# Forgetting attention in a hybrid decoder block: maxima from one product, scores with keys on partitions

## The chip, the cores and the metric

The kernel is one program on one core of one Trainium2 chip. The metric is the device time of one execution in microseconds; shown are the median of three runs and one execution recorded by the hardware profiler. In the profile PE is the matrix engine, PEld its weight loads, DVE the vector engine, ACT the scalar engine, POOL the GpSimd engine and SP the engine that issues the DMAs.

## The reference

One decoder layer on x of shape (1, 2048, 1024) in float32. A normalised input is projected once, and the columns feed three branches: attention with forget gates (8 heads of 64), a chunked state-space branch, and a gated linear recurrence. Their outputs (512 + 1024 + 512 columns) are joined, multiplied by `w_out` (2048 x 1024) and added to x. What the change touches:

```python
q, k = rms_norm(q, q_g), rms_norm(k, k_g)            # per head, 64 wide
c = jnp.cumsum(log_f, axis=1)                        # one number per head and position
logits = q_i @ k.T * 64**-0.5 + (c_i[:, None] - ck[None, :])
logits = jnp.where(kpos <= qpos, logits, -jnp.inf)
o = jax.nn.softmax(logits) @ v
y_att = o * jax.nn.silu(z_att)
h = x + concat([y_att, y_ssd, y_lru]) @ w_out
```

## The kernel before

All large products are in float32r, which the kernel makes accurate by splitting an operand into a rounded part (`h`) and the rest (`l`) and adding products of the parts. The stages, in order of time: load and normalise x (transposed, split: `uh`, `ul`); projections of the state-space inputs with their convolution; the recurrence branch; the scan of the state-space branch beside the attention projections (`pqk`, `pvz`); attention; the last products with `w_out`. Results that a later stage needs go through DRAM (`qk_d`, `v_d`, `za_d`, `c_d`, `at_d`).

Attention works in units of one head `h` and 256 queries (`sb`, 0 to 7; 64 units, heads one after the other). A unit has sb+1 key pairs `kp` of 256 keys, so 36 per head and 288 in all. For a unit:

- `logits` (lines 855 to 905) takes each of its two blocks of 128 queries with queries on the partitions. For every chunk of up to 512 keys it makes two products (L880, L881: queries' large and small parts against both parts of the keys, stacked on the partitions), 320 chunks in all. A DVE instruction (L883) adds the cumulative gate, writes the logits to SBUF and keeps the running minimum of the negated logits; the diagonal chunk has its causal mask put on the gate rows by POOL (L875). One long exponential on ACT (L886) then runs over the whole row and gives the row sum.
- `attend` (lines 907 to 966) turns the probabilities by PE transposes of 128x128 (L936, 1088 in all) into PSUM, splits them into `ph` (ACT, L943) and `pl` (DVE, L944), and multiplies by the split values (L922, L923). At the end of a unit the result, head rows on partitions, is copied out, transposed back (L960), its two halves added and multiplied by the gate divided by the row sum (POOL, L913, L963, L964), and stored to `at_d` with positions as rows.
- The products of the next unit's logits are put between the key pairs of this unit.

The products with `w_out` are a generator, `sweeps`, with 512 steps of three products of 512 columns (L1006 to L1008, tile `po`). `fill` gives 260 of them to attention, about 0.9 after each key pair, and 12 to its start; they may come up to `LAG` = 4 pairs early. The other 240 steps follow attention. `mix` loads the left operand of a step; for the attention part it transposes what it reads from `at_d` (L984) before it splits it.

The order of instructions on each engine is fixed when the program is built, by a scheduler that works with estimated times and these priorities; on the chip every engine, and SP's queue of DMAs, runs in order.

The projection of values and attention gate (`group_vz`) makes products of 256 columns for head pairs 1 to 3 (L338, L340, L342) and of 280 for pair 0, with positions on partitions.

Of the kernel before, what the change touches and what calls it, by code (L numbers as in the profile page):

```python
# [13 lines left out]
ALU = mybir.AluOpType  # L14
# [23 lines left out]
AHEAD = 1  # L38
NDV = 3
# [7 lines left out]
def hybrid_block(ctx, tc, x, norm_g, w_in, q_norm_g, k_norm_g, forget_b, ssd_conv_w, ssd_conv_b,  # L47
# [16 lines left out]
    am = ctx.enter_context(tpool(name="am", bufs=4))  # L64
# [7 lines left out]
    v_d = [dram(f"v_d{p}", [S, 2, P]) for p in range(4)]  # L72
    za_d = [dram(f"za_d{p}", [S, P]) for p in range(4)]
# [6 lines left out]
    c_d = dram("c_d", [8, NT, P])  # L80
    gt_d = [dram(f"gt_d{g}", [4, P, S]) for g in range(2)]
    at_d = dram("at_d", [S, 512])
# [266 lines left out]
    def proj_ch(w, m, tb, name):  # L349
        wh, wl, n = w  # L350
        ps = psj.tile([P, 512], F32, name=name, tag="pj")
        ms = slice(m * P, m * P + P)
        for k in range(KD):
            T.matmul(ps, wh[k][:, ms], uh[tb][k], start=(k == 0), stop=False)  # L354
            T.matmul(ps, wh[k][:, ms], ul[tb][k], start=False, stop=False)  # L355
            T.matmul(ps, wl[k][:, ms], uh[tb][k], start=False, stop=(k == KD - 1))  # L356
        return ps


    def group_vz(pool, vpool, p):  # L360
        cols = [(C_V + p * P, P), (C_ZA + p * P, P)]
        if p == 0:
            cols += [(C_F, 8), (C_DT, 16)]
        w = weights(cols)
        for t2 in range(8):
            vs = vpool.tile([P, 2, 2, P], F32R, name=f"vs{p}_{t2}", tag="qk")
            zt = pool.tile([P, 2, P], F32, name=f"zt{p}_{t2}", tag="zt")
            if p == 0:
                pss = [proj_tok(w, t2 * 2 + i, f"pvz{p}_{t2 * 2 + i}")[:, 0:280].unsqueeze(1)
                       for i in range(2)]  # L370
            else:
                pss = [proj_tok2(w, t2, f"pvz{p}_{t2}")]
                if p == 3 and t2 == 4:
                    anchor[1] = anchor[0]
            m = 2 // len(pss)
            for j, ps in enumerate(pss):
                ii = slice(j * m, j * m + m)
                pv = ps[:, :, 0:P].rearrange("p i (h d) -> p i h d", d=64)
                A.activation(vs[:, ii, :, 0:64], pv, AF.Copy, scale=0.5)
                V.scalar_tensor_tensor(vs[:, ii, :, 64:128], pv, 0.5,  # L380
                                       vs[:, ii, :, 0:64].bitcast(F32), op0=ALU.mult,
                                       op1=ALU.subtract)
                th = (ap1 if p else pool).tile([P, m, P], F32, name=f"th{p}_{t2}_{j}",
                                               tag="sqq")
                A.activation(th, ps[:, :, P:2 * P], AF.Tanh, scale=0.5)
                V.scalar_tensor_tensor(zt[:, ii, :], th, 1.0, ps[:, :, P:2 * P], op0=ALU.add,
                                       op1=ALU.mult)
                if p == 0:
                    V.tensor_copy(etot[:, t2 * 2 + j, 0:8], ps[:, 0, 256:264])
                    V.tensor_copy(dt[:, t2 * 2 + j, :], ps[:, 0, 264:280])  # L390
            rr = slice(t2 * 256, t2 * 256 + 256)
            dma(v_d[p][rr].rearrange("(i p) h c -> p i (h c)", p=P),
                vs.bitcast(F32).rearrange("p i h c -> p i (h c)"))
            dma(za_d[p][rr, :].rearrange("(i p) c -> p i c", p=P), zt)
# [16 lines left out]
    def gates(g1):  # L411
# [62 lines left out]
        for t in range(NT):  # L474
            dma(c_d[:, t, :], cr[t * 8:(t + 1) * 8, :])
# [3 lines left out]
    with tpool(name="cl", bufs=1) as cl, tpool(name="g1", bufs=1, side="right") as g1:  # L479
        for gq in range(6):  # L480
            if gq == 1:

                group_vz(g0, g0, 0)
# [250 lines left out]
    cx = ExitStack()  # L734
    kvA = cx.enter_context(tpool(name="kvA", bufs=1, side="right"))
    kq = cx.enter_context(tpool(name="kq", bufs=2, side="right"))
    heads = {}
    units = [(h, sb) for h in range(8) for sb in ORD[h]]

    def load_head(h):  # L740
# [3 lines left out]
        kh = pool.tile([P, S], F32R, name=f"kh{h}", tag="kh")  # L744
        vv = pool.tile([P, NT, P], F32R, name=f"vv{h}", tag="vv")
        cb = pool.tile([P, S], F32, name=f"cb{h}", tag="cb")
        dma(cb, c_d[h:h + 1].rearrange("h t l -> h (t l)").partition_broadcast(P))
        dma(kh[0:64, :].bitcast(F32), qk_d["k", "h", p][hs, :])
        dma(kh[64:128, :].bitcast(F32), qk_d["k", "l", p][hs, :])
        dma(vv.bitcast(F32), v_d[p][:, b, :].rearrange("(t p) c -> p t c", p=P))  # L750
        heads[h] = [kh, vv, cb]


    def load_q(h, sb):
        p, b = divmod(h, 2)
        hs = slice(b * 64, b * 64 + 64)
        qh = kq.tile([P, 512], F32R, name=f"qh{h}_{sb}", tag="qh")
        ql = kq.tile([P, 512], F32R, name=f"ql{h}_{sb}", tag="ql")
        sb -= sb % 2
        qs = slice(sb * 256, sb * 256 + 512)  # L760
        for u in range(2):
            dma(qh[u * 64:u * 64 + 64, :].bitcast(F32), qk_d["q", "h", p][hs, qs])
            dma(ql[u * 64:u * 64 + 64, :].bitcast(F32), qk_d["q", "l", p][hs, qs])
        heads[h][3:] = [qh, ql]
# [30 lines left out]
    with tpool(name="ap", bufs=2) as pool, tpool(name="ap1", bufs=1) as ap1, \  # L795
            tpool(name="qkp", bufs=QB) as qkp:
        for p in range(4):
# [37 lines left out]
            if p > 0:  # L835
                group_vz(pool, qkp, p)
            if p == 2:
                load_head(0)
                load_q(*units[0])
# [4 lines left out]
    a4 = cx.enter_context(tpool(name="a4", bufs=4))  # L844
    o2 = cx.enter_context(tpool(name="o2", bufs=2))
    o3 = cx.enter_context(tpool(name="o3", bufs=LEAD))
    a2 = cx.enter_context(tpool(name="a2", bufs=2))
    a3 = cx.enter_context(tpool(name="a3", bufs=3))
    kvB = cx.enter_context(tpool(name="kvB", bufs=1))
# [3 lines left out]
    psP = pcx.enter_context(tpool(name="psP", bufs=PB[3], space=PSUM))  # L853

    def logits(h, sb):

        sm = a2.tile([P, 2], F32, name=f"sm{h}_{sb}", tag="sm")
        u = {"L": [], "sm": sm}
        steps = []

        def chunk(i, c0):
            kh, vv, cb, qh, ql = heads[h]
            u["vv"] = vv
            qt = sb * 2 + i
            n = (qt + 1) * P
            w = min(512, n - c0)
            if c0 == 0:
                u["L"].append(a4.tile([P, S], F32, name=f"L{h}_{qt}", tag="L"))
                u["mx"] = am.tile([P, 1], F32, name=f"mx{h}_{qt}", tag="mx")
            lt, mx = u["L"][i], u["mx"]  # L870
            last = c0 + w == n
            cc = cb[:, c0:c0 + w]
            if last:
                cm = a2.tile([P, 512], F32, name=f"cm{h}_{qt}", tag="cm")
                G.affine_select(out=cm[:, 0:w], in_=cc, pattern=[[-1, w]], compare_op=ALU.is_ge,  # L875
                                fill=-NEG, base=w - P, channel_multiplier=1)
                cc = cm[:, 0:w]
            qs = slice((sb % 2) * 256 + i * P, (sb % 2) * 256 + i * P + P)
            ps = psS.tile([P, 512], F32, name=f"S{h}_{qt}_{c0}", tag="S")
            T.matmul(ps[:, 0:w], qh[:, qs], kh[:, c0:c0 + w], start=True, stop=False)  # L880
            T.matmul(ps[:, 0:w], ql[:, qs], kh[:, c0:c0 + w], start=False, stop=True)  # L881

# [233 lines left out]
```

## Time and profile before

| | us |
|---|---|
| median of 3 runs (2053.45 to 2055.52) | 2053.6 |
| the profiled execution | 2056.6 |
| its span, first to last instruction | 2054.9 |
| PE busy in the span | 1997.6 |
| DVE busy | 1255.9 |
| ACT busy | 978.7 |
| POOL busy | 536.7 |

A busy time is the union of an engine's instructions. Matmuls are pipelined and their ends are modelled, so the time that a matmul costs is read from the distance between the starts of two that follow each other, not from its listed duration.

### The profile page before, as it was taken

What the parts mean: (1) busy time and instruction counts of PE and PEld (TensorE: products, weight loads), DVE (VectorE), ACT (ScalarE), POOL (GpSimd) and SP (SyncE); (2) the same over time, 40 slices, a digit from 0 to 9 for tenths busy, and PEclk for the clock granted to TensorE, in tenths of its full rate; (3) what the DMA queues carried; (4) which work ended last, traced back from release to release, by engine and by line L of the source; (5) the groups of instructions that cost most, each with busy time, mean ns of one, the idle gap of its engine ahead of it and who ended that gap; (6) DMA issues with size and microseconds to landing.
All of it is one profiled execution on the core that took longest, in us unless ns stands there. A gap on an engine that the chain in (4) does not pass through costs nothing. (4 is left out here: it accounts for less than half of the span.)

```text
span 2054.9 us, 36001 instructions
## 1 busy us (share of the span) xinstructions
PE 1997.6 (97%) x12517; PEld 1756.5 (85%) x12517; DVE 1255.9 (61%) x2676; ACT 978.7 (48%) x2049; POOL 536.7 (26%) x798
## 2 busy tenths in 40 slices
PE   7999999999999999898999999899999999999999
PEld 6898888898989898787888998788887888888887
DVE  5848555664554646767666255576776776784333
ACT  6624444444443534444445244466665666663110
POOL 0100000222232414455552001253333333323110
PEclk9999999999999999999999999999999999999999
DMA  5322223121212145667656646475476366442443
GB/s 187 85 74 70 63 82 96 44 73 32 83 39 87 30 123 162 187 179 209 196 160 182 179 143 194 142 204 161 135 188 174 113 181 169 119 136 86 134 143 118
DMA packets 287317, 265.18 MB, mean 129 GB/s; under 512 B 59780, under 2 KB 227232, under 8 KB 285088
## 3 DMA queue, kind: packets, MB, share of 16 engines
q1 hardware_dynamic: 286976, 262.85, 43.8%
q8 instruction: 99, 1.62, 0.3%
q0 software_dynamic: 160, 0.03, 0.1%
q14 instruction: 82, 0.67, 0.1%
HBM read 168.22 MB, written 94.57 MB: 128 GB/s over the span
## 5 line engine op out<-in xcount | busy, mean ns | idle before, releaser
L944 DVE TENSOR_TENSOR pl<-T,ph 128x512 fp32r<-128x512 f32 (+2 forms) x352 | 191.3, 565 | 71.4 <-ACT ph L943 69.7
L1006 PE MATMUL po<-woh,mh 128*128 128x512 f32 x512 | 213.2, 416 | 10.4 <-DVE xr L1014 6.6
L943 ACT CAST ph<-T 128x512 fp32r<-128x512 f32 (+2 forms) x352 | 161.6, 490 | 125.2 <-PE T L936 86.4
L1007 PE MATMUL po<-wol,mh 128*128 128x512 f32 x512 | 202.0, 395 | 0.0
L1008 PE MATMUL po<-woh,ml 128*128 128x512 f32 x512 | 201.2, 398 | 0.0
L936 PE MATMUL T<-ident,L 128*128 128x128 f32 x1088 | 171.5, 274 | 3.1 <-ACT L L886 2.1
L886 ACT ACTIVATE L<-L,mx 128x1920 f32<-128x1920 f32 (+15 forms) x128 | 154.5, 1207 | 40.6 <-DVE mx L883 36.5
L354 PE MATMUL pxx<-uh,wh 128*128 128x512 f32 x384 | 153.7, 402 | 2.2 <-ACT uh L299 2.1
L922 PE MATMUL O<-ph,vv 128*128 128x256 f32 x576 | 153.7, 288 | 0.6 <-ACT ph L943 0.5
L355 PE MATMUL pxx<-ul,wh 128*128 128x512 f32 x384 | 153.0, 400 | 0.0
L923 PE MATMUL O<-pl,vv 128*128 128x256 f32 x576 | 152.0, 288 | 0.5 <-DVE pl L944 0.3
L356 PE MATMUL pxx<-uh,wl 128*128 128x512 f32 x384 | 151.2, 396 | 0.0
L342 PE MATMUL pqk<-wh,ul 128*128 128x256 f32 x512 | 151.1, 295 | 0.0
L338 PE MATMUL pqk<-wh,uh 128*128 128x256 f32 x512 | 150.3, 294 | 0.0
L340 PE MATMUL pqk<-wl,uh 128*128 128x256 f32 x512 | 146.1, 285 | 0.0
L340 PE MATMUL pzs<-wl,uh 128*128 128x256 f32 x512 | 143.6, 281 | 0.0
L342 PE MATMUL pzs<-wh,ul 128*128 128x256 f32 x512 | 143.3, 280 | 0.0
L407 DVE SCALAR_TENSOR_TENSOR accx<-rtx,cv,accx 128x512 f32<-128x512 f32 x144 | 108.1, 752 | 57.4 <-ACT accx L404 54.4
L338 PE MATMUL pzs<-wh,uh 128*128 128x256 f32 x512 | 143.0, 281 | 0.0
L674 ACT ACTIVATE ab<-ab,nacs 128x128 f32<-128x128 f32 x256 | 82.1, 391 | 121.6 <-POOL ab L670 121.5
L936 PEld LDWEIGHTS T<-ident,L 128*128 128x128 f32 x1088 | 126.7, 141 | 14.3 <-ACT L L886 6.1
L875 POOL TENSOR_SCALAR_AFFINE_SELECT cm<-cb 128x384 f32<-128x384 f32 (+3 forms) x128 | 58.6, 460 | 298.5 <-DVE mx L883 144.6
(319 smaller groups left out, 5587.6 us busy)
## 6 DMA issues: line engine op xcount, KB each, us to landing
ab<-acs_d SPq DMA_DIRECT2D x64, 256.0 KB
pt_d<-xr SPq DMA_DIRECT2D x64, 256.0 KB
wr<-in_w_in_dram SPq DMA_DIRECT2D x192, 64.0 KB
wr<-in_w_in_dram SPq DMA_DIRECT2D x80, 128.0 KB
xt<-in_x_dram SPq DMA_DIRECT2D x16, 512.0 KB
xs_d<-stx SPq DMA_DIRECT2D x32, 256.0 KB
v_d<-vs SPq DMA_DIRECT2D x32, 256.0 KB
zs_d<-zs SPq DMA_DIRECT2D x32, 256.0 KB
```

The lines of the kernel that those rows point to most:

```text
L338: T.matmul(ps[:, i, :], h[k][:, sl], wh[k], start=(k == 0 and i == 0), stop=False, skip_group_check=True)
L340: T.matmul(ps[:, i, :], h[k][:, sl], wl[k], start=False, stop=False, skip_group_check=True)
L342: ins = T.matmul(ps[:, i, :], l[k][:, sl], wh[k], start=False, stop=last, skip_group_check=True)
L354: T.matmul(ps, wh[k][:, ms], uh[tb][k], start=(k == 0), stop=False)
L886: A.activation(lt[:, 0:n], lt[:, 0:n], AF.Exp, bias=mx, scale=-1.0, accum_out=sm[:, i:i + 1])
L922: T.matmul(po[:, ca], vv[:, kt, :], ph[:, jj, ca], start=(kt == 0), stop=False)
L936: ins = T.transpose(pt[:, jj, i * P:(i + 1) * P], L[i][:, kt * P:(kt + 1) * P], ident)
L943: A.copy(ph[:, ja, ca], pt[:, ja, ca])
L944: V.tensor_tensor(pl[:, ja, ca], pt[:, ja, ca], ph[:, ja, ca].bitcast(F32), op=ALU.subtract)
L1006: T.matmul(ps, mh[:, j, :], h, start=(j == 0), stop=False)
L1007: T.matmul(ps, mh[:, j, :], l, start=False, stop=False)
L1008: T.matmul(ps, ml[:, j, :], h, start=False, stop=(j == 3))
```

## The change

Queries and keys change places. The main steps:

- The row maxima come from one product per chunk instead of two, of the large parts only. The gate is part of that product: two rows of the keys' operand `k2` hold the split cumulative gate (`c_d` now holds both parts), against rows of ones in the queries' operand `q3`. A row of minus ones in `k2` and a row of `q3` for the maximum are used later. DVE reduces each chunk straight from PSUM (`maxima`); the diagonal chunk is masked by adding a constant tile.
- `flip` transposes the two columns of maxima of a unit and ACT writes them as rows into `q3`.
- `score` makes, for each key pair, the logits again with keys on partitions: two products of 256 query columns per 128 keys (`k2` with `q3`, and `kx` with `qx` for the small parts), minus the maximum; the diagonal pair gets its mask by one more product. ACT takes the exponential from PSUM, pair by pair, and copies the rounded part `ph`; DVE makes `pl`; POOL adds the probabilities up in `acc`. At the end of the unit POOL folds the sum to 256 columns, ACT and POOL split it.
- `av` multiplies by the values three pairs later (`AVL` = 3), and `finish`, one pair after the unit's last `av`, makes the row sums by two products with ones, adds the halves (ACT, DVE), multiplies by the gate (POOL) and stores heads and positions transposed. The row sums go to DRAM; in the last head they are read back, inverted and stored.
- `mix` for the attention part reads the transposed result and a broadcast of the inverse sums, and multiplies on DVE; its transposes are gone.
- `group_v` (values, two groups of 256 columns) and `group_za` (gate, transposed, products of 512 columns) replace `group_vz`.

The diff, cut to its core:

```diff
-    def logits(h, sb):
...
-    def attend(h, sb, u, steps, fill):
...
+    def maxima(j):
...
+        def first():
+            if j % 2 and j + 1 < len(units):
+                load_q(j + 1)
...
+        def chunk(i, c0):
...
+            T.matmul(ps[:, 0:w], q3[0:96, o:o + P], k2[0:96, c0:c0 + w], start=True, stop=True)
+            to = col if nc_ == 1 else u["mc"][:, c0 // 512:c0 // 512 + 1]
+            if c0 + w == n:
+                jk = a1.tile([P, 512], F32, name=f"jk{j}_{i}", tag="jk")
+                V.tensor_tensor_reduce(jk[:, 0:w], ps[:, 0:w], zm[:, 640 - w:640], 1.0, 3.0e38,
+                                       ALU.add, ALU.min, to)
+                if nc_ > 1:
+                    V.tensor_reduce(col, u["mc"][:, 0:nc_], axis=AX.X, op=ALU.min)
+            else:
+                V.tensor_reduce(to, ps, axis=AX.X, op=ALU.min)
...
+    def flip(j):
...
+        pm = psS.tile([P, P], F32, name=f"pm{j}", tag="S")
+        T.transpose(pm[0:97, :], mzs[j % 2][:, 0:97], ident)
+        A.copy(q3[96:97, o:o + P], pm[64:65, :])
+        A.copy(q3[96:97, o + P:o + 256], pm[96:97, :])
+
+    def score(j, kp):
...
+        for jj in range(2):
+            ks = slice((kp * 2 + jj) * P, (kp * 2 + jj + 1) * P)
+            qs = slice(o + P if last and jj else o, o + 256)
+            ps = pt[:, 256 * jj:256 * jj + qs.stop - qs.start]
+            T.matmul(ps, k2[:, ks], q3[:, qs], start=(jj == 0), stop=False, skip_group_check=True)
+            ins = T.matmul(ps, kx[:, ks], qx[:, qs], start=False, stop=True, skip_group_check=True)
+        if last:
+            pv = pt.rearrange("p (a b) -> p a b", b=256)[:, :, 0:P]
+            ins = T.matmul(pv, idr, zmt.unsqueeze(1).broadcast_to([P, 2, P]), start=False,
+                           stop=True, skip_group_check=True)
+        e = a4.tile([P, 512], F32, name=f"e{j}_{kp}", tag="e")
+        A.activation(e[:, 0:n], pt[:, 0:n], AF.Exp, scale=-1.0)
...
+        A.copy(ph[:, 0:n], e[:, 0:n])
+        V.tensor_tensor(pl[:, 0:n], e[:, 0:n], ph[:, 0:n].bitcast(F32), op=ALU.subtract)
...
+                G.tensor_tensor(u["acc"], u["acc"], e, op=ALU.add)
...
+            G.tensor_tensor(w, u["acc"][:, 0:256], u["acc"][:, 256:512], op=ALU.add)
+            G.tensor_tensor(w, w, e[:, 0:256], op=ALU.add)
...
+        G.tensor_tensor(w[:, P:256], w[:, P:256], e[:, 256:384], op=ALU.add)
...
+        A.copy(u["ah"], w[:, 0:256])
+        G.tensor_tensor(u["al"], w[:, 0:256], u["ah"].bitcast(F32), op=ALU.subtract)
...
+    def finish(j):
...
+        T.matmul(po[:, 256:512], onr, u["ah"], start=False, stop=False, skip_group_check=True)
+        T.matmul(po[:, 256:512], onr, u["al"], start=False, stop=True, skip_group_check=True)
...
+        A.copy(tm, po[64:128, :])
+        V.tensor_tensor(to, po[0:64, 0:256], tm[:, 0:256], op=ALU.add)
+        G.tensor_tensor(to, to, u["za"], op=ALU.mult)
...
+        dma(at_d[p][b * 64:b * 64 + 64, cs], to)
...
+        dma(s_d[qt, h:h + 1, :].rearrange("i o t -> o i t"),
+            tm[0:1, 256:512].rearrange("o (i t) -> o i t", i=2))
+        if h == 7:
+            sr = a2.tile([16, P], F32, name=f"sr{j}", tag="sr")
+            dma(sr, s_d[qt].rearrange("i h t -> (i h) t"))
+            V.reciprocal(sr, sr)
+            dma(r_d[qt].rearrange("i h t -> (i h) t"), sr)
...
         if kind == "att":
-            dma(mt.rearrange("p i c -> p (i c)"), at_d[tsl, :])
-            src = pso["X"].tile([P, 4, P], F32, name=f"px{t}_{k0}", tag="X")
-            for i in range(4):
-                T.transpose(src[:, i, :], mt[:, i, :], ident)
-            A.copy(mh, src)
-            V.tensor_tensor(ml, src, mh.bitcast(F32), op=ALU.subtract)
+            dma(mt, at_d[:, :, tsl].rearrange("i p t -> p i t"))
+            rb = o2.tile([P, 4, P], F32, name=f"rb{t}", tag="xr")
+            for b in range(2):
+                dma(rb[b * 64:b * 64 + 64, :, :],
+                    r_d[t].rearrange("(i b) t -> b i t", b=2)[b:b + 1].partition_broadcast(64))
+            V.tensor_tensor(mt, mt, rb, op=ALU.mult)
+            A.copy(mh, mt)
+            V.tensor_tensor(ml, mt, mh.bitcast(F32), op=ALU.subtract)
...
+    for i in range(len(tasks) + AVL + 1):
+        ins = None
+        if i < len(tasks):
+            ins = score(*tasks[i])
+            if i in flips:
+                flip(flips[i])
+            for f in at.get(i, ()):
+                f()
+        if 0 <= i - AVL < len(tasks):
+            av(*tasks[i - AVL])
+        if i > AVL:
+            j, kp = tasks[i - AVL - 1]
+            if kp == units[j][1]:
+                finish(j)
+        if ins is not None:
+            fill(ins)
```

`at` spreads the chunks of `maxima` of a unit over the pairs of the unit before; `flips` puts a unit's `flip` beside the last pair of the unit before. The tiles `e` have four buffers, `ph` and `pl` five, the score tiles in PSUM three, the tiles of `po` one as before.

More of the change, by code (lines that the diff above doesn't have):

```diff
@@ L38 @@
 AHEAD = 1
+AVL = 3
 NDV = 3
@@ L375, in group_vz @@
[L375 to L390, printed above, removed]
@@ new lines, in group_za @@
+    def group_za(pool, vpool, g):
+        w = weights([(C_ZA + g * 256, 256)])
+        for tb in range(4):
+            for mm in range(2):
+                m = g * 2 + mm
+                ps = proj_ch(w, mm, tb, f"pza{m}_{tb}")
+                if g == 1 and tb == 2 and mm == 0:
+                    anchor[1] = anchor[0]
+                th = pool.tile([P, 512], F32, name=f"th{m}_{tb}", tag="sqq")
+                A.activation(th, ps, AF.Tanh, scale=0.5)
+                zt = vpool.tile([P, 512], F32, name=f"zt{m}_{tb}", tag="qk")
+                V.scalar_tensor_tensor(zt, th, 1.0, ps, op0=ALU.add, op1=ALU.mult)
+                dma(za_d[m][:, tb * 512:(tb + 1) * 512], zt)
@@ L853, in hybrid_block @@
     psP = pcx.enter_context(tpool(name="psP", bufs=PB[3], space=PSUM))
-    def logits(h, sb):
-        sm = a2.tile([P, 2], F32, name=f"sm{h}_{sb}", tag="sm")
-        u = {"L": [], "sm": sm}
-        steps = []
[L861 to L881, printed above, removed]
-            V.tensor_tensor_reduce(lt[:, c0:c0 + w], ps[:, 0:w], cc, 1.0,
-                                   3.0e38 if c0 == 0 else mx, ALU.add, ALU.min, mx)
-            if last:
-                A.activation(lt[:, 0:n], lt[:, 0:n], AF.Exp, bias=mx, scale=-1.0,
-                             accum_out=sm[:, i:i + 1])
@@ L889, in first @@
+    make_k2(1)
+    U = [{} for _ in units]
+    def maxima(j):
+        h, sb = units[j]
+        u = U[j]
+        steps = []
         def first():
-            j = units.index((h, sb))
-            if j % 2 == 0 and j > 0:
-                load_q(h, sb)
-            za = a2.tile([P, 2, 64], F32, name=f"za{h}_{sb}", tag="za")
+            if j % 2 and j + 1 < len(units):
+                load_q(j + 1)
+            za = a3.tile([64, 256], F32, name=f"za{j}", tag="za")
             u["za"] = za
@@ new lines, in av @@
+    def av(j, kp):
+        h, sb = units[j]
+        u = U[j]
+        vv = heads[h][2]
+        if kp == 0:
+            u["O"] = psO.tile([P, 512], F32, name=f"O{j}", tag="O")
+        po = u["O"]
+        ph, pl = u.pop(kp)
+        for jj in range(2):
+            kt = kp * 2 + jj
+            qs = slice(P if kp == sb and jj else 0, 256)
+            cs = slice(256 * jj, 256 * jj + 256 - qs.start)
+            T.matmul(po[:, qs], vv[:, kt, :], ph[:, cs], start=(kt == 0), stop=False,
+                     skip_group_check=True)
+            T.matmul(po[:, qs], vv[:, kt, :], pl[:, cs], start=False, stop=(kt == 2 * sb + 1),
+                     skip_group_check=True)
@@ L1059, in hybrid_block @@
     with tc.high_priority(offset=HP), tc.issue_after(anchor[1].ins):
-        cur, steps = logits(*units[0])
+        steps = maxima(0)
         for j, st in enumerate(steps):
@@ L1075, in fill @@
                 next(filler)
[L1077 to L1080 removed]
+    tasks = [(j, kp) for j, (h, sb) in enumerate(units) for kp in range(sb + 1)]
+    begin = [tasks.index((j, 0)) for j in range(len(units))]
+    at = {}
+    for j in range(1, len(units)):
+        a, b = max(0, begin[j - 1] - 1), begin[j] - 1
+        st = maxima(j)
+        for i, f in enumerate(st):
+            at.setdefault(a + i * (b - a) // len(st), []).append(f)
+    flips = {begin[j] - 1: j for j in range(1, len(units))}
+    for i in range(len(tasks) + AVL + 1):
[14 more added lines that the diff above has]
+            fill(ins)
     pcx.close()
[L1082 to L1083 removed]
+    pso["P"] = cx.enter_context(tpool(name="psP2", bufs=6, space=PSUM))
+    pso["X"] = True
     for _ in filler:
```

243 lines of the change are left out of this document (136 added, 107 removed).

## The prediction

> **What bounds the kernel now.** First the page: the span, how busy PE is, the chain that ended last, and the group that the change breaks up.
>
> ```profile
> span 2054.9 us, 36001 instructions
> ...
> PE 1997.6 (97%) x12517; PEld 1756.5 (85%) x12517; DVE 1255.9 (61%) x2676; ACT 978.7 (48%) x2049; POOL 536.7 (26%) x798
> ...
> PE 43%; DVE 2%; DMA 2%; issue 1%; ACT 1%; POOL 0%; SPq 0%; DVEq 0%; POOLq 0%; ACTq 0%
> ...
> L886 ACT ACTIVATE L<-L,mx 128x1920 f32<-128x1920 f32 (+15 forms) x128 | 154.5, 1207 | 40.6 <-DVE mx L883 36.5
> ```
>
> PE is busy nearly throughout, and the chain names it above all others, so the time is first of all a count of matmuls. Next, the busy times by stage: attention, and what follows it.
>
> ```profile
> 1292.00:1885.00 593.00, 582.67 (x3706) 509.83 (x3705) 428.12 (x1164) 370.09 (x770) 205.64 (x407) 0.99 0.53 150
> 1885.00:2055.00 170.00, 165.72 (x756) 135.75 (x756) 56.40 (x132) 16.61 (x28) 17.14 (x14) 1.00 0.39 132
> ```
>
> The columns are length, then PE, PEld, DVE, ACT and POOL busy, then clock and DMA. In the 593 us of attention PE is idle for 10 us, at a clock of 0.99; DVE is busy 72%, ACT 62%, POOL 35%. The 170 us after it are products with w_out alone. What a matmul costs there is read from starts in PE's timeline (start, then listed duration):
>
> ```profile
> 1303.52 0.28 PE L922 MATMUL O<-ph,vv 128*128 128x256 f32 x1
> ...
> 1304.58 0.28 PE L923 MATMUL O<-pl,vv 128*128 128x256 f32 x1
> 1304.70 0.60 PE L936 MATMUL T<-ident,L 128*128 128x128 f32 x4
> 1305.05 0.48 PE L1006 MATMUL po<-woh,mh 128*128 128x512 f32 x1
> 1305.37 0.40 PE L1007 MATMUL po<-wol,mh 128*128 128x512 f32 x1
> 1305.60 0.40 PE L1008 MATMUL po<-woh,ml 128*128 128x512 f32 x1
> ```
>
> Ten products of 256 columns start between 1303.52 and 1304.70: 0.118 us each. One of 512 takes 0.23 (1305.37 to 1305.60). The four transposes and the two products after them take 0.90 up to 1305.60; less 2 x 0.23 that is 0.111 for a transpose of 128, nearly the price of 256 columns. The first product behind them starts late, so the transposes' own starts alone would make them too cheap.
>
> **The change on PE.** Counts follow from the loops; these rows confirm the two largest.
>
> ```profile
> L936 PE MATMUL T<-ident,L 128*128 128x128 f32 x1088 | 171.5, 274 | 3.1 <-ACT L L886 2.1 <-DVE pl L944 0.8
> ...
> L881 PE MATMUL S<-kh,ql 128*128 128x512 f32 x224 | 88.9, 397 | 0.0
> ```
>
> Removed:
> - the second product of 320 chunks: 224 x 0.23 + 32 x (0.173 + 0.118 + 0.111) = 64.4;
> - 1088 transposes of probabilities x 0.111 = 120.8;
> - two transposes per unit, 128 x 0.111 = 14.2;
> - in the products after attention 4 x 16 transposes = 7.1;
> - 768 projections of 256 columns become 384 of 512: 90.6 - 88.3 = 2.3.
>
> Sum 208.8. Added:
> - scores, four products per pair, 1152, of which 128 are half as wide: 1024 x 0.118 + 128 x 0.111 = 135.0;
> - the mask, 64 x 0.118 = 7.6;
> - the transpose of the maxima, 64 x 0.111 = 7.1;
> - row sums, 128 x 0.118 = 15.1.
>
> Sum 164.8. Net: PE has 44.0 us less to do, 35 of them in attention. The products with values stay at 1152, the steps with w_out at 512. Two of these have no row. A product over 96 partitions instead of 128 could be cheaper by a quarter (320 x up to 0.06 = 18 less) or not at all; I take not at all, as the rows show a price by columns. The mask product reads its operand repeated and writes in two pieces: 0.118, at most 0.23, so 7 more.
>
> **The change on DVE.** Rows for a read of PSUM with one operand in SBUF, for two operands in SBUF while POOL works, and for two in SBUF over twice the columns:
>
> ```profile
> L944 DVE TENSOR_TENSOR pl<-T,ph 128x512 fp32r<-128x512 f32 x224 | 148.8, 687 | 58.8 <-ACT ph L943 57.4
> ...
> L690 DVE TENSOR_TENSOR y<-y,yo 128x512 f32<-128x512 f32 x30 | 25.3, 845 | 0.5
> ...
> L621 DVE TENSOR_TENSOR XC<-XC,MM 128x1024 f32<-128x1024 f32 x8 | 9.8, 1226 | 6.4 <-ACT MM L618 6.3
> ```
>
> The 320 reductions of chunks stay 320 reads of PSUM of the same widths: 0. `pl` now reads both operands from SBUF: between 0.613 (half of 1.226) and 0.845 instead of 0.687, so for 224 full ones -17 to +35. New are 64 additions of 256 columns at the end of units, some 0.42 each (an estimate from half of 0.687), 27 us, and 96 very short reductions of at most 0.26, 25 us. DVE goes from 428 to between 463 and 515.
>
> **The change on ACT.**
>
> ```profile
> L943 ACT CAST ph<-T 128x512 fp32r<-128x512 f32 x224 | 123.6, 588 | 66.4 <-PE T L936 60.6 <-PE O L922 3.0 <-DVE pl L944 1.6
> ...
> L956 ACT COPY os<-O 128x256 f32<-128x256 f32 x64 | 23.6, 368 | 23.1 <-PE O L923 22.5 <-ACT L L886 0.2
> L993 ACT CAST mh<-mt 128x512 fp32r<-128x512 f32 x36 | 22.3, 621 | 15.7 <-PE po L1007 8.2 <-DMA kh<-kh_d 2.5 <-DMA mt<-gt_d 2.4
> L943 ACT CAST ph<-T 128x128 fp32r<-128x128 f32 x64 | 16.8, 263 | 31.6 <-DVE pl L944 31.5
> ```
>
> Gone: the long exponentials, 154.5, and two copies per unit, 128 x 0.368 = 47. New: 288 exponentials from PSUM, priced as the cast from PSUM, 224 x 0.588 + 64 x 0.46 = 161, up to a fifth more; `ph` from SBUF, 224 x (0.621 - 0.588) = 7; `tm`, 64 x 0.588 = 38; `ah`, 64 x 0.368 = 24; two rows of maxima per unit, 128 x at most 0.263 = 34. Net +62 to +94: ACT goes from 370 to 432 to 464.
>
> **The change on POOL.** It gets the sums of probabilities:
>
> ```profile
> L994 POOL TENSOR_TENSOR ml<-mt,mh 128x512 fp32r<-128x512 f32 x48 | 62.0, 1292 | 202.2 <-ACT mh L993 178.7 <-PE O L922 13.6 <-PE pf L960 4.4
> ...
> L682 POOL TENSOR_TENSOR xs<-xs,drow 128x512 f32<-128x512 f32 x32 | 35.4, 1108 | 0.3
> L192 POOL TENSOR_TENSOR wl<-wr,wh 128x256 fp32r<-128x256 f32 x32 | 32.2, 1010 | 121.9 <-ACT wh L191 121.8
> ...
> L963 POOL TENSOR_TENSOR ats<-fs 128x128 f32<-128x128 f32 x64 | 29.4, 460 | 116.9 <-ACT fs L962 97.9 <-DMA at_d<-ats 16.9 <-DVE sm L910 1.1
> ...
> L583 POOL TENSOR_TENSOR ZZ<-tzl,ZZ 128x512 f32<-128x512 f32 x16 | 21.4, 1342 | 0.4
> ```
>
> A head has 21 additions of 512 columns to `acc`: 168 x 1.108 to 1.342 = 186 to 225. Folding, in 56 units: twice 256 columns, at 0.676 (on the line from 0.460 to 1.108) to 1.010, and once 128 at 0.460: 101 to 139; 8 x 0.46 = 4 in the rest. The split `al` and the gate, 64 each of 256 columns: 86 to 130. The splits for w_out in the stage, 35 x 1.292 = 45. POOL goes from 206 to between 422 and 543.
>
> **Waits.** With PE's 35 us gone, attention would take 558. DVE would be busy 83 to 92% of that, ACT 77 to 83%, POOL 76 to 97%: the covers are thinner than before. A product with values now comes three pairs behind its scores, the score tiles in PSUM have three buffers and are read by ACT alone, and `finish` comes four pairs behind the last score, some 7 us: I cost these at nothing, hidden by PE's work on pairs in between. A pair is 0.47 for scores, 0.47 for values, 0.9 x 3 x 0.23 = 0.62 for w_out and 0.2 for chunks of maxima, 1.8 in all.
>
> What is late next is the first score of a unit. It waits for its maxima: the last reduction 0.69, a short one 0.26, the transpose 0.27 (its listed duration), two casts 0.53, and one instruction ahead on DVE (0.69) and one on ACT (0.59): 3.0 us. Ahead of it on PE's queue stand the values and w_out of one pair; behind it everything else. A long unit before it covers that. Where the unit before has one or two pairs (16 of 64), 3.0 - 1.8 = 1.2 us is open: 19 us. The old kernel had the same kind of chain through L883, L886 and L936 and yet lost little, so nothing is the lower bound; 64 units x 1.2 = 77 the upper. I take 19, since the rows say that most units are long.
>
> `load_q` now writes one of two fixed tiles, free only when the unit two before has made its last score; in seven heads the unit between has one pair, 1.8 us. The queue rows, from SP's own list of waits, show what a wait for a DMA costs it:
>
> ```profile
> SPq L1027 <- DMA pt_d<-xr: 62.6, 45, 4.2
> ```
>
> At 4.2 each that is 7 x 2.4 = 17, at the mean of 1.4 nothing. I take nothing. The last head adds, per unit, a store of sums, a read back and a store: 8 x 3 x 1.4 = 34 us in which SP's queue stands, with loads for w_out behind it. These are asked for one tile of eight steps ahead, some 16 us, so nothing; without that cover the first steps after attention wait once, 3 x 4.2 = 13. Three DMAs for queries instead of four and the two rows of gates instead of a broadcast are lighter: nothing.
>
> **Sum.** The profiled execution took 2056.6, 1.7 over its span; the median is 2053.6, 3.0 under it. Its own time less 44 plus 19 is 2031.6; for the median, 2053.6 - 44 + 19 = 2029.
>
> **The rivals.**
>
> *Slower: POOL waits for ACT within each unit's fold.* `ah` on ACT follows POOL's fold, `al` on POOL follows `ah`, and both engines run in order; behind `ah` on ACT stand the next exponentials, behind `al` the next additions, and the four buffers of `e` come free only with them. POOL's waits for a copy by ACT:
>
> ```profile
> POOL ats L963 <- ACT fs L962: 97.9, 41, 7.0
> ```
>
> That is 2.4 us each; 64 x 2.4 = 153. With POOL's middle, 480, the stage would be 633, with its lowest 575, which PE hides. It decides from 593 + 9 = 602 on (9 is what PE saves outside attention). Halfway between 602 and 633 the time is 2053.6 - 9 + 25 = 2070. Against it: these old waits were idle time of an engine with nothing to do, and `al` has four pairs.
>
> *DVE and POOL shut each other out.* L690 takes 0.845 beside a busy POOL, where L621 needs 0.613 for as many columns. If `pl` and POOL exclude each other entirely, their least prices add: 224 x 0.613 + 64 x 0.46 = 167, and 422, together 589. Attention then takes 589 instead of 593: 2053.6 - 9 - 4 = 2041, and with 3% of gaps 2058. The Trainium skill ("SBUF — State Buffer", section "SBUF: two separate sides") states such a rule: a DVE instruction with two SBUF operands and a GpSimd instruction that reads SBUF hold one pair of ports in turn, each for its whole length. The two rows agree in direction; that POOL's instructions at 1.108 were not all uncontended themselves speaks against the full sum.
>
> *All of it arrives.* No new wait, and the 10 us of idle time go as well: 2053.6 - 44 to 54, so 2000 to 2010, up to 2016. For it: values now have three pairs of slack instead of one. Against it: three engines above 75%.
>
> **How the numbers follow.** The forecast (2016 to 2041) 0.43; all of it (2000 to 2016) 0.18; exclusion (2041 to 2058) 0.15; POOL and ACT (2058 to 2085) 0.22; others 0.02. A measurement of this kernel tells 0.2%, 4 us, from no change. Faster: 0.43 + 0.18 + 0.06 of exclusion, 0.67; same: its other 0.09; slower: 0.22 + 0.02. The range, 2005 to 2072, leaves out a third of the full gain's chance and less than half of the slow case's. The forecast's own range is 2016 to 2041.
>
> **What would show it.** Right: 576 fewer matmuls in all (11941), attention near 577, scores and values starting 0.118 apart, PE's idle time in front of the first score of short units, released by ACT. Wrong: POOL near 95% with ACT's `ah` waiting for it (the slow rival); `pl` at 0.85 or more and POOL's additions over 1.3 (exclusion); DVE ahead of PE in the chain; PE waiting for the loads of queries. What would break the forecast is a PE that is no longer the engine others wait for.

## The result and the profile after

The changed kernel takes 2213.9 us (median of 4 runs, 2201.7 to 2218.6), the kernel before 2054.6 beside it: ratio 1.0765, 95% interval 1.0725 to 1.0805. It is 159 us slower; the forecast was 2029, and the range ended at 2072. From the page of the changed kernel: span, busy times, the chain by engine and by line, and two groups (busy time, mean ns, idle time before).

```profile
span 2200.0 us, 34666 instructions
...
PE 2048.2 (93%) x11941; PEld 1762.5 (80%) x11941; DVE 1433.3 (65%) x2513; ACT 1019.2 (46%) x2113; POOL 880.2 (40%) x898
...
PE 18%; DVE 9%; POOL 4%; issue 3%; DMA 2%; ACT 2%; SPq 0%; DVEq 0%; POOLq 0%; ACTq 0%
DVE pl L986 5%; PE po L1095 4%; PE po L1096 4%; PE po L1097 4%; PE T L974 2%; PE T L975 2%; POOL ac L996 1%; DVE mc L942 1%; PE S L932 1%; PE O L1026 1%; DVE jk L937 1%; DMA at_d<-to 1%; ACT e L982 1%; POOL w L1001 1%; POOL w L1000 1%
...
L986 DVE TENSOR_TENSOR pl<-e,ph 128x512 fp32r<-128x512 f32 (+1 forms) x288 | 338.2, 1197 | 46.4 <-ACT ph L985 46.2
...
L996 POOL TENSOR_TENSOR ac<-ac,e 128x512 f32<-128x512 f32 x120 | 185.9, 1549 | 23.2 <-ACT e L982 16.1
```

The 11941 matmuls are those predicted. The chain covers only part of the span, 49% before and 38% now; of what it covers PE had 43 of 49 before and has 18 of 38 now, and its costliest line is now `pl` on DVE. The mean of `pl`, 1197 ns, mixes 512 and 384 columns; by form, the full ones take 1299. The windows of attention and of what follows, columns as before:

```profile
1285.00:2040.00 755.00, 649.12 (x3592) 546.59 (x3592) 591.48 (x1024) 415.88 (x863) 528.52 (x493) 0.92 0.40 110
2040.00:2200.00 160.00, 155.51 (x687) 128.47 (x685) 63.40 (x145) 16.80 (x27) 15.84 (x12) 1.00 0.51 158
```

All of the loss lies in attention, 755 us instead of 593, with PE idle for 106 of them and at a granted clock of 0.92 instead of 0.99. What follows is shorter than before, 160 instead of 170, and so is what precedes it, 1285 instead of 1292. The list of waits (engine, tile and line, releaser: us, times, longest) of attention and its start names the candidates:

```profile
ACT ah L1007 <- POOL w L1004: 125.1, 46, 5.7
...
PEld O L1026 <- DVE pl L986: 73.2, 99, 3.1
...
PE O L1026 <- DVE pl L986: 47.9, 68, 2.9
```

And the timeline (start, length of the group of instructions) shows `pl` beside POOL's additions:

```profile
1641.32 6.23 POOL L996 TENSOR_TENSOR ac<-ac,e 128x512 f32<-128x512 f32 x4 [0.85 <-ACT e L982]
...
1642.93 5.18 DVE L986 TENSOR_TENSOR pl<-e,ph 128x512 fp32r<-128x512 f32 x3
```

Three `pl` take 5.18 us while POOL adds without a pause, and four additions take 6.23. One after the other, by the least prices of the prediction, they would take 3 x 0.613 + 4 x 1.108 = 6.27. But 1.108 is the price of another POOL instruction; the same additions take 1.30 where `pl` is out of their way (e1), and with 1.30 the sum is 7.04, against 5.2 for the four additions alone. So the two run nearly in turn, with a part of each overlapped.

So three theories: A, `pl` and POOL's additions shut each other out, and PE waits for `pl`; B, ACT's `ah` waits for POOL's fold (125 us, the larger wait); C, the new products cost PE more than priced.

### The profile page after: what moved, and what is told of

Its sections match the earlier page's. It is cut to its first block, busy times and chain, and to the rows that moved or that the text cites. A ratio compares the mean times of both kernels' runs of the same rounds, so it can differ in the third digit from the quotient of the medians.

```text
span 2200.0 us, 34666 instructions
## 1 busy us (share of the span) xinstructions
PE 2048.2 (93%) x11941; PEld 1762.5 (80%) x11941; DVE 1433.3 (65%) x2513; ACT 1019.2 (46%) x2113; POOL 880.2 (40%) x898
## 5 line engine op out<-in xcount | busy, mean ns | idle before, releaser
L986 DVE TENSOR_TENSOR pl<-e,ph 128x512 fp32r<-128x512 f32 (+1 forms) x288 | 338.2, 1197 | 46.4 <-ACT ph L985 46.2
L1026 PE MATMUL O<-pl,vv 128*128 128x256 f32 x576 | 162.9, 313 | 48.8 <-DVE pl L986 47.9
L982 ACT ACTIVATE e<-T 128x512 f32<-128x512 f32 (+1 forms) x288 | 162.8, 575 | 85.5 <-PE T L975 48.4
L996 POOL TENSOR_TENSOR ac<-ac,e 128x512 f32<-128x512 f32 x120 | 185.9, 1549 | 23.2 <-ACT e L982 16.1
L1026 PEld LDWEIGHTS O<-pl,vv 128*128 128x128 f32 x576 | 114.8, 199 | 76.3 <-DVE pl L986 73.2
L974 PE MATMUL T<-q,k 128*128 128x256 f32 x576 | 163.2, 305 | 12.9 <-ACT q L958 12.5
L942 DVE TENSOR_REDUCE mc<-S 128x1 f32<-128x512 f32 x192 | 129.9, 682 | 57.8 <-PE S L932 57.6
L985 ACT CAST ph<-e 128x512 fp32r<-128x512 f32 (+1 forms) x288 | 165.3, 597 | 2.8 <-PE O L1024 0.6
L1083 POOL TENSOR_TENSOR ml<-mt,mh 128x512 fp32r<-128x512 f32 x48 | 67.1, 1399 | 244.1 <-ACT mh L1082 244.0
L975 PE MATMUL T<-qx,kx 128*128 128x256 f32 x576 | 156.6, 299 | 0.0
```

The lines of the kernel that those rows point to most:

```text
L974: T.matmul(ps, k2[:, ks], q3[:, qs], start=(jj == 0), stop=False, skip_group_check=True)
L975: ins = T.matmul(ps, kx[:, ks], qx[:, qs], start=False, stop=True, skip_group_check=True)
L982: A.activation(e[:, 0:n], pt[:, 0:n], AF.Exp, scale=-1.0)
L985: A.copy(ph[:, 0:n], e[:, 0:n])
L986: V.tensor_tensor(pl[:, 0:n], e[:, 0:n], ph[:, 0:n].bitcast(F32), op=ALU.subtract)
L996: G.tensor_tensor(u["acc"], u["acc"], e, op=ALU.add)
```

## The experiments

### Where the 159 us went: e1 to e4

**e1_pl_psum.** `pl` takes its first operand from the score tile in PSUM instead of `e` in SBUF; everything else stays, so POOL has the same work.

```diff
-        V.tensor_tensor(pl[:, 0:n], e[:, 0:n], ph[:, 0:n].bitcast(F32), op=ALU.subtract)
+        V.tensor_tensor(pl[:, 0:n], pt[:, 0:n], ph[:, 0:n].bitcast(F32), op=ALU.min)
```

> DVE's instruction for pl takes its first operand from the score tile in PSUM instead of e in SBUF (and the smaller of the two instead of their difference, to keep numbers finite): the values are not those of the reference, the number and width of instructions and all of POOL's work stay. Theory A (pl and POOL's additions shut each other out, because both read two operands from SBUF): pl falls from 1.20 us on average to about 0.69, POOL's additions from 1.48 to 1.1 to 1.3, PE's 121 us of waits for pl nearly vanish, time 2030 to 2100. Theory B (ACT's ah waits 125 us for POOL's fold and holds up what is behind it): pl changes little in what PE waits for, time 2150 or more. Theory C (the new products cost PE more than their starts say): time stays within 20 of 2202.

2114.3 us (one run), 100 less, a little short of the 2030 to 2100 expected by theory A. Its page, and PE's waits:

```profile
L986 DVE TENSOR_TENSOR pl<-T,ph 128x512 fp32r<-128x512 f32 (+1 forms) x288 | 186.3, 655 | 67.5 <-ACT ph L985 66.9
...
L996 POOL TENSOR_TENSOR ac<-ac,e 128x512 f32<-128x512 f32 x120 | 155.5, 1296 | 33.1 <-ACT e L982 29.0
```

```profile
PEld O L1026 <- DVE pl L986: 10.7, 17, 1.3
```

One operand moved to the other memory takes `pl` from 1197 to 655 and POOL's additions from 1549 to 1296 at once, and PE's weight loads wait 10.7 us for `pl` instead of 73.2. Theory A holds.

**e2_no_sums.** The same conflict, taken away on POOL's side: the 168 additions to `acc` go. The row sums are then those of the last two key pairs alone, and eight short DVE instructions, left out of the diff here, keep them above zero.

```diff
-            if kp == 0:
-                u["acc"] = e
...
-                G.tensor_tensor(u["acc"], u["acc"], e, op=ALU.add)
+            u["acc"] = e
             return ins
```

> The 168 additions of probabilities into acc on POOL are left out (the row sums are then those of the last two key pairs, so the output is not the reference's; a guard keeps them above zero); the fold, ah and al stay. Theory A: with POOL's work halved pl falls to 0.65 to 0.80, time 2030 to 2090, close to the run with pl from PSUM. Theory B: the fold is no longer late, ah's wait for POOL falls from 125 to under 40 us, time 2030 to 2090 too; the two are told apart by the other runs. Theory C: within 20 of 2202.

2142.5 us (one run), 71 less.

```profile
L986 DVE TENSOR_TENSOR pl<-e,ph 128x512 fp32r<-128x512 f32 (+1 forms) x288 | 218.9, 775 | 70.9 <-ACT ph L985 70.3
```

`pl` falls with its own instruction unchanged, to a mean inside theory A's 0.65 to 0.80, because POOL has less to read. The time missed that theory's 2030 to 2090: the folds and `al` remain on POOL, and `pl` stays above e1's 655. The same cause, from the other side.

**e3_ah_early.** Theory B: `ah` is copied from the last `e`, ahead of POOL's fold, so that ACT never waits for POOL there.

```diff
+        A.copy(u["ah"], e[:, 0:256])
         if sb > 0:
             w = a2.tile([P, 256], F32, name=f"w{j}", tag="w")
...
-        A.copy(u["ah"], w[:, 0:256])
```

> ah is copied from the last pair's e, ahead of the fold, so ACT does not wait for POOL (al = w - ah still makes the sum whole); the rest is unchanged. Theory A: ACT's 125 us of waiting go, but pl stays at 1.1 us or more and PE goes on waiting for it: time 2150 to 2200. Theory B: time 2050 to 2100. Theory C: within 20 of 2202.

2219.2 us (one run): no gain, even 19 us over what theory A expected. The largest wait of the list is gone from it, and the time is where it was; PE still waits for `pl`:

```profile
PEld O L1026 <- DVE pl L986: 62.7, 91, 4.0
```

Theory B falls. ACT stands elsewhere instead: over the whole span its waits for PE ahead of `q` grew from 72.1 to 125.7, and those ahead of `tm` from 23.2 to 81.4.

**e4_exp_in_psum.** The conflict removed with the computation kept: the exponential is written in place in PSUM, `ph` and `pl` read it there, and POOL sums `ph`, the rounded value that PE uses.

```diff
-        A.activation(e[:, 0:n], pt[:, 0:n], AF.Exp, scale=-1.0)
+        A.activation(pt[:, 0:n], pt[:, 0:n], AF.Exp, scale=-1.0)
...
-        A.copy(ph[:, 0:n], e[:, 0:n])
-        V.tensor_tensor(pl[:, 0:n], e[:, 0:n], ph[:, 0:n].bitcast(F32), op=ALU.subtract)
+        A.copy(ph[:, 0:n], pt[:, 0:n])
+        V.tensor_tensor(pl[:, 0:n], pt[:, 0:n], ph[:, 0:n].bitcast(F32), op=ALU.subtract)
+        e = ph.bitcast(F32)
```

> The exponential is written back into the score tile in PSUM, ph and pl are made from it there, and POOL adds up the rounded ph from SBUF instead of e (row sums of the rounded part). pl keeps one operand in SBUF. Theory A: pl about 0.69, POOL's additions 1.1 to 1.3, time 2030 to 2100 although the score tiles are held longer. Theory B: ah still waits for the fold, 2150 or more. Theory C: within 20 of 2202.

2115.3 us (median of 2), ratio to before 1.0292 (1.0224 to 1.0359): 98.6 us of the 159 are gone, somewhat less than theory A had promised, as in e1.

```profile
L985 DVE TENSOR_TENSOR pl<-T,ph 128x512 fp32r<-128x512 f32 (+1 forms) x288 | 186.3, 655 | 68.9 <-ACT ph L984 65.9
...
L996 POOL TENSOR_TENSOR ac<-ac,ph 128x512 f32<-128x512 f32 x120 | 155.8, 1299 | 14.6 <-ACT ph L984 9.2
```

`pl` and POOL both read the tile `ph` here, at the speed of e1, so it was not that they shared a tile. But 61 us are still lost against before. The waits of attention in this kernel:

```profile
PE pm L956 <- DVE mz L940: 27.8, 22, 4.8
```

```profile
ACT tm L1042 <- DMA s_d<-tm: 30.1, 6, 6.7
```

The six waits of ACT lie in six heads, each 12 to 16 us behind the loads of the next head. One of them in the timeline, SP's queue first:

```profile
1351.23 7.36 SPq L1047 DMA_DIRECT2D at_d<-to  x1
```

```profile
1363.66 0.58 ACT L1042 COPY tm<-O 64x512 f32<-64x512 f32 x1 [6.70 <-DMA s_d<-tm]
```

```profile
1350.00:1370.00 20.00, 14.78 (x72) 12.24 (x70) 9.59 (x25) 8.97 (x20) 8.92 (x14) 0.83 0.80 185
```

Five loads of the next head are issued up to 1350.64. The store behind them, normally 0.5 us, takes 7.36 to issue (in the other five heads it is a load of queries that stands there, for 6.5 to 9.3 us); the store of the sums stands behind it; `tm` has two buffers, so ACT stands 6.70 in front of the next `tm`, and the exponentials of units that begin stand behind `tm`. PE is busy 14.78 of 20 us, at a clock of 0.83. Two theories for the rest: S, this queue; F, the flip chain (maxima on DVE, transpose on PE, two copies on ACT) ahead of each unit's first score.

### Where the other 61 us went: e5 to e8

**e5_tm_bufs.** e4 with four buffers for `tm` and `to`.

```diff
-        tm = a2.tile([64, 512], F32, name=f"tm{j}", tag="tm")
-        to = a2.tile([64, 256], F32, name=f"to{j}", tag="to")
+        tm = a4.tile([64, 512], F32, name=f"tm{j}", tag="tm")
+        to = a4.tile([64, 256], F32, name=f"to{j}", tag="to")
```

> The kernel with the exponential in place in PSUM (2115.3 us), with four buffers instead of two for tm and to. In its trace ACT stood 30.1 us in front of tm for the store of an earlier tm, six times 6.7 us, at the heads' starts, and a store of at_d took 7.36 us to issue on SP behind the next head's loads. Theory S (stores held up on SP stop ACT, and ACT stops the exponentials and flips behind tm): the 30 us of ACT's wait go, and with a clock that falls less after the gaps, 2075 to 2095. Theory F (the flip chain, from the row maxima on DVE over PE's transpose to the two copies on ACT, holds every unit's first score; the stores stand beside it): 2105 to 2118.

2077.4 us, ratio 1.0107 (1.0079 to 1.0136): 37.9 less than e4, as theory S said. How long the stores of `at_d` took to issue (least/median/most, ns), and who waited for the store of the sums:

```profile
L1047 SPq DMA_DIRECT2D at_d<-to x64: 458/494/7327, 1289.7 to 1910.2; - x64
```

```profile
  ACT tm L1042: 3.1, 1
```

The slow issue is still there, 7.3 us; the buffers only keep ACT from standing behind it. PE's waits for `mz`, 27.8 in e4, fell too, though nothing of the flip was changed:

```profile
PE pm L956 <- DVE mz L940: 10.3, 19, 2.0
```

**e6_load_later.** e4 with the next head's loads at the sixth unit of a head instead of the third.

```diff
-            if j % 8 == 2 and h < 7:
+            if j % 8 == 5 and h < 7:
```

> The same kernel (2115.3 us) with the next head's loads issued three units later, away from the short units that begin a head. Theory S: SP's queue is free when the short units store, so the 30.1 us of ACT's wait before tm go, or move to where units are long and cost little: 2075 to 2100. Theory F: 2105 to 2118.

2116.1 us, ratio 1.0284 (1.0255 to 1.0313): no gain over e4, the number of theory F. But the block is not gone, it moved with the loads:

```profile
ACT tm L1042 <- DMA s_d<-tm: 30.7, 5, 8.3
```

So what theory S forecast here failed, 2075 to 2100 with the waits gone or cheap; but the block that it names is still there, with the same wait of ACT. The remedy missed it: it isn't the short units that make the block. That five loads at once make it is tried in e9.

**e7_maxima_early.** e4 with the maxima two pairs and the flip one pair earlier (a third `q3` tile and more buffers of `qx`; the loads go one unit later, to keep their place in the order).

```diff
-        a, b = max(0, begin[j - 1] - 1), begin[j] - 1
+        a, b = max(0, begin[j - 1] - 3), begin[j] - 3
...
-    flips = {begin[j] - 1: j for j in range(1, len(units))}
+    flips = {begin[j] - 2: j for j in range(1, len(units))}
```

> The same kernel (2115.3 us) with each unit's row maxima two pairs earlier and its flip one pair earlier (a third q3 tile, a third qx buffer; the next head's loads stay at the same place in the order). Theory F: PE's waits for mz in front of pm (27.8 us, 22 of them) and for ACT's q in front of the first scores (10.8 us, 25 of them) go, and the time comes to 2065 to 2085. Theory S: the gaps are made by ACT standing in front of tm, and a flip that is issued earlier stands behind it in the same way: 2100 to 2118.

2093.5 us, ratio 1.0188 (1.0169 to 1.0207): 21.8 less than e4, between the two expectations. PE's waits for `mz` in front of `pm` shrank from 27.8 to 5.0, those for `q` in front of the first scores from 10.8 to at most 1.1, and a new one took part of their place, the PSUM bank of `pm` being held until ACT has copied it; the block at `tm` stayed:

```profile
PE S L936 <- ACT q L962: 30.7, 26, 5.9
```

```profile
ACT tm L1046 <- DMA s_d<-tm: 38.9, 6, 7.7
```

**e8_all.** All of these: exponential in PSUM, three buffers for `tm` and `to`, loads at the sixth unit, maxima and flips earlier.

> All of it together: exponential in place in PSUM, three buffers for tm and to, head loads later, maxima and flips earlier. If exclusion, stores and flip chain are the whole of the gap, PE has nothing left to wait for: 2015 to 2045, which is 10 to 40 below the kernel before. If PE's own work costs more than the sum of my prediction (2010 to 2029), or the granted clock stays at 0.86 to 0.95 in the attention with PE busy, it stops at 2060 to 2090, and the change can't win by mending waits.

2072.5 us, ratio 1.0079 (1.0058 to 1.0101). That is the number of the second case, a PE that can't win, but not by its reason, as e9 and e11 show. The two gains don't add: 37.9 and 21.8 alone, 42.8 together. One gap, in the timeline of SP and of DVE and in the windows, shows what is left:

```profile
1363.92 6.47 SPq L1053 DMA_DIRECT2D s_d<-tm  x1
```

```profile
1377.62 0.42 DVE L1110 TENSOR_TENSOR xr<-xr,po 128x256 f32<-128x256 f32 x1 [5.70 <-DMA mt<-lr_d]
```

```profile
1370.00:1380.00 10.00, 3.63 (x25) 3.21 (x23) 3.68 (x10) 1.70 (x5) 4.99 (x6) 0.88 0.87 220
```

SP's queue still stands 6.5 us behind the five loads. ACT no longer cares; now DVE does, in front of an `xr` of the products with w_out. The row names the load `mt<-lr_d`, which was issued at 1375.50, behind the store that stood; a load of an `xr`, at 1373.58, was too. The maxima stand behind that `xr`, and PE waits 6.37 us for them. It is busy for 3.63 of 10 us. A queue that blocks finds the next engine to block.

### The queue itself, and a version below before: e9 to e12

**e9_loads_spread.** e8 with the five loads spread over five units (the keys and their gate rows in the first, the values in two halves).

```diff
-            if j % 8 == 5 and h < 7:
-                load_head(h + 1)
+            if j % 8 >= 3 and h < 7:
+                load_head(h + 1, j % 8 - 3)
```

> The kernel with all four edits (2072.5 us) with the next head's loads no longer issued together but one for each of five units (the values in two halves). In its trace 1360 to 1370 had a DMA share of 0.92, one store took 6.47 us to issue on SP, an xr on DVE stood 5.7 us for a load that came after it, and PE 6.4 us for the maxima behind that xr. Theory S (SP's queue full at heads' starts): seven heads by some 6 us, with the clock that falls after it: 2025 to 2060. Theory P (PE is near its own sum, its many short waits remain): 2065 to 2075.

2059.3 us (median of 10), ratio 1.002 (1.0004 to 1.0037): 13.2 below e8, just inside what theory S expected. The longest issue of a store of the sums, 6.47 us in e8, is now 1.83:

```profile
L1061 SPq DMA_DIRECT2D s_d<-tm x64: 585/602/1831, 1291.9 to 1890.3; - x64
```

But the queue is not free of blocks. The longest issue of any DMA in attention falls from 9.02 to 4.13, that of a load behind a head whose loads were still issued within 8 us (1421 to 1429):

```profile
1429.94 4.13 SPq L1094 DMA_DIRECT2D mt<-lr_d  x1
```

**e10_values_later.** The products with values 4 pairs behind the scores (six buffers for `ph` and `pl`); to make room, `tm` and `to` go back to two buffers.

```diff
-AVL = 3
+AVL = 4
```

> The same with loads spread, two buffers for tm and to again, and the products with the values 4 pairs behind the scores instead of 3 (six buffers for ph and pl). Theory P: PE's waits for pl in front of the products with values, 7.5 + 3.7 us in the kernel with all four edits, go: 5 to 15 us below the kernel with loads spread. If SP is relieved, the third buffer of tm and to is not missed; if it is, the time is 10 to 30 above it.

2082.4 us, ratio 1.0125 (1.0105 to 1.0145): 23 above e9, inside the 10 to 30 expected if the third buffer is missed.

```profile
ACT tm L1054 <- DMA s_d<-tm: 27.4, 5, 6.9
```

ACT's wait for the store is back. In one of its five places (6.44 us, up to 1436.01) the queue still blocks: the store of the sums is issued at 1433.50, behind this load:

```profile
1428.23 5.18 SPq L1094 DMA_DIRECT2D mt<-lr_d  x1
```

In the other four no issue took over 2.8 us, and the store lands late all the same: one issued by 1597.26 lets ACT go on at 1601.92. So it isn't the issue alone that the third buffer covers. What `AVL` alone does stays open: two things were altered in one run.

**e11_banks.** e9 with three PSUM banks for the maxima and two for the scores.

```diff
-PB = (2, 3, 2, 1)
+PB = (3, 2, 2, 1)
```

> The same as the kernel with loads spread, with three PSUM banks for the maxima and two for the scores, instead of two and three. PE waited 20 us for the copies q before it could start a product of the maxima (the bank of pm). If these waits hold PE, the time falls by 5 to 20 us; if the scores' banks do, since ph and pl now read them to the end, it rises by 30 or more.

2050.5 us (median of 9), ratio to before 0.9976 (0.996 to 0.9993): 8.8 below e9, as expected for the bank of `pm`, and the one version faster than before, by 0.24%, less than what single runs of either kernel differ by. Its attention and what follows, and PE's largest wait in attention:

```profile
1292.00:1887.00 595.00, 561.42 (x3556) 502.15 (x3557) 437.74 (x1014) 422.81 (x857) 449.42 (x501) 0.97 0.50 140
1887.00:2050.00 163.00, 159.14 (x703) 131.51 (x701) 66.79 (x150) 17.42 (x28) 16.82 (x13) 0.99 0.49 155
```

```profile
PE S L944 <- DMA q<-qh_d: 12.3, 9, 3.8
```

The waits for `q` on ACT are gone from the top; the largest is now for the loads of queries. Its three longest, 3.85, 3.46 and 2.32 us, each follow a block of SP's queue, the first this one:

```profile
1427.10 6.96 SPq L813 DMA_DIRECT2D qx<-qh_d  x1
```

```profile
1441.06 0.77 PE L944 MATMUL S<-k,q 96*128 96x512 f32 x1 [3.85 <-DMA q<-qh_d]
```

The loads of the next head, spread over five units in the code, were issued within 4 us there (1421.57 to 1425.4). So the fastest version still has the blocked queue, and what a queue without it would give was not run.

**e12_after_spread.** The changed kernel as it was given, with the loads spread and nothing else.

> The changed kernel as it was given (2213.9 us), with nothing altered but the next head's loads spread over five units. Theory A (pl and the additions of POOL shut each other out, which is about 100 of the 159 us): 2180 to 2205. If the loads at the heads' starts make the long pl and the rest follow from that: under 2150.

2216.9 us (median of 2), ratio 1.0782 (1.0756 to 1.0808): no gain at all, not even the 10 to 30 us that theory A allowed.

```profile
L994 DVE TENSOR_TENSOR pl<-e,ph 128x512 fp32r<-128x512 f32 (+1 forms) x288 | 338.9, 1200 | 49.8 <-ACT ph L993 49.5
```

The likely reading is that the queue hides behind `pl` as long as this takes 1200. It isn't shown cleanly, since this run's queue still has issues of 5.86 and 5.21 us, where the changed kernel has six of 5.0 to 8.0. With e5 to e9 it fits losses in layers: each shows its price only when the one above it is gone. In order: exclusion 98.6; the stores that stop ACT 37.9 (e4 to e5); the flips and the rest 4.9 (e5 to e8); loads in one block 13.2; banks 8.8. Together 163.4, which is 2213.9 less 2050.5. The order sets the shares, as e7 shows.

## Why the prediction was wrong, step by step

**"The change on PE"** held. The count is exact, scores and values start 0.118 apart, and PE's attention work, busy time by clock, went from 582.7 x 0.99 = 577 to 561.4 x 0.97 = 545 in e11: 32 less where 35 were predicted. This is rough: the clock is a mean, and listed times grow where PE has gaps, so the same product gives 649.1 x 0.92 = 597 for the changed kernel itself. Theory C falls as the cause of the 159 us: a kernel with the same 11941 matmuls, e11, takes 5 us less than the kernel before.

**"The change on DVE"** is the step that failed. `pl` was set between 0.613 and 0.845 and took 1.299 at 512 columns. DVE in attention came to 591 instead of 463 to 515; in e11, with `pl` from PSUM, it is 438. The upper bound, 0.845, was read as the price beside a busy POOL, but it is the mean of a row that mixes two cases. The row's least, middle and longest in ns, before the change:

```profile
L690 DVE TENSOR_TENSOR y<-y,yo x30: 678/693/1386, 788.8 to 1122.3; 128x512 f32<-128x512 f32 x30
```

Of the 30, 17 took no more than 0.693 us, 11 of them with no POOL instruction beside them; the longest, 1.386, had two of POOL's beside it without a pause. This kernel has POOL at work for most of attention. A pair of instructions that take turns has an upper bound of the one plus the other, 0.613 + 1.108 = 1.721, or 1.91 with 1.30 for the addition; the three `pl` above took 1.73 each.

**"The change on POOL"**: additions at 1.108 to 1.342 took 1.549, and 1.30 in e1 and e4, where `pl` has an operand in PSUM. POOL's 528 us in attention lie inside 422 to 543, so the sum gave no warning. (ACT came to 416, under its 432 to 464.)

**"DVE and POOL shut each other out"** was the right mechanism, with the signs that the prediction had listed for it (`pl` over 0.85, additions over 1.3), and the wrong price: 2041 to 2058 predicted, 13 us less to 4 more than before, some 99 us measured. It was costed as throughput, 167 + 422 = 589 in a stage of 593, therefore nearly free. But an exclusive resource asked for 99% of the stage can only be free if nothing else delays either side. DVE has some 250 us of other work (591 less `pl`'s 338) in order with `pl`, and POOL waits for ACT's `ah`; while one of them does something else, the pair stands unused. An estimate: with POOL's 449 us of e11 in place of the least price of 422, the two ask for 167 + 449 = 616 us, 23 more than the old stage, while the stage took 162 more. So most of the loss is not throughput. What fits is latency: `pl` arrives late, PE's products with values stand (e1 takes most of these waits away), and the clock falls; how the 99 us divide between these is not shown. The Trainium skill ("SBUF — State Buffer", section "SBUF: two separate sides") calls the shared ports an exclusive lock that is held for the whole instruction, with the other side fully blocked. The runs e1 and e2 agree with an exclusion, and the stretch above nearly with its full length: 1.73 for a `pl` against the 1.91 of one instruction behind the other.

**"POOL waits for ACT within each unit's fold"**: the wait came, as ACT's 125 us for POOL, and cost nothing (e3).

**"Waits"** failed in the second place. `finish` and its stores were costed at nothing and the two buffers of `tm` were never looked at, nor who stands behind ACT's `tm`: 37.9 us. The loads of a head were not looked at, beyond the gate rows being lighter, though the stores behind them on SP had become what ACT and DVE wait for. The kernel before issues four of them over 15 to 24 us, and no issue in its attention takes over 2.6 us; the changed kernel issues five within 3 to 4 us, and the DMA behind them stands for 5.0 to 8.0. The flip chain was set at 19 us, and moving it earlier gave 21.8 (e7). That nearness is in part luck: the buffers of e5 alone cut the waits for `mz` from 27.8 to 10.3, so much of them was ACT standing at `tm`. `load_q`, set at 0 for the reuse of its tiles, cost little of that kind: in the changed kernel PE's products wait 2.1 us for it. The 12.3 us of e11 are another thing, the blocked queue.

**What is left** between e11 and the forecast, 21 us: PE is idle for 33.6 us of its attention, where it was for 10.3 before. PE's two largest waits there are the 12.3 us for loads of queries and, in front of the scores, 10.0 for `pl`, which must free one of only two score banks. The rest, short waits and the clock of 0.97, was not taken apart.

## What to carry to other kernels

Before work is moved to POOL, or a DVE operand from PSUM to SBUF, list which DVE instructions would read two operands from SBUF beside it, and cost each with a whole POOL instruction in front of it, in the path of whoever waits for the result, not as a sum over the stage. The longest wait in a list is not the one that costs: ask who stands behind the waiting engine, as the 125 us that e3 removed for nothing show. When a wait is mended and the time doesn't move, look for a second one under it, and for a blocked DMA queue look at what was issued just ahead of it: buffers moved the block to another engine, moving the loads moved the block in time, and spreading them shortened it where they were spread in time and not only in the code. Check that in SP's timeline, for every DMA and not for one store.

## What the runs showed of the hardware

- A DVE instruction with two operands in SBUF took 1.73 us beside POOL additions without a pause, and 1.299 on the mean of all 224 full ones; with one operand in PSUM, 0.685 under the same POOL work (e1), and POOL's additions fell from 1.549 to 1.30.
- The DMA behind five loads in one block took 6.5 to 9.3 us to issue on SP in e4 (a store of `at_d` takes 0.50 in the middle of the 64). With the loads spread in the code the longest issue was 4.13 us in e9, 5.18 in e10 and 6.96 in e11, each behind loads that were still issued within 4 to 8 us. What stood ahead is shown; that it is the cause rests on e6, where the block moved with the loads, and e9.
- Two stretches of 10 and 20 us in which PE had gaps show a granted clock of 0.88 (e8) and 0.83 (e4), and the next 10 and 20 us 0.77 and 0.91, so a gap cost more than its own length there.
